# Dealing the two groups of head pairs in turn over the slots of a recurrent mixer

## The chip, the core and the metric

The kernel runs on one core of a Trainium2 chip. The core has five engines with a queue each: TensorE (PE in the profile, with its weight loads as PEld), VectorE (DVE), ScalarE (ACT), GpSimd (POOL) and SyncE (SP), which here only issues DMAs. Each engine works through its instructions in a fixed order and stands where one has to wait. The metric is the time of one execution on the device, in microseconds (us).

## What is computed

A trunk of two layers over 256 tokens of width 1024. Each layer runs three token mixers on the same normalised input and merges them:

```python
for l in range(DEPTH):
    h = rmsnorm(x, norm_g[l])
    proj = h @ w_in[l]
    (a_q, a_ff, a_fb, a_i, a_g, b_q, b_k, b_v, b_g, c_s, c_g, merge) = jnp.split(proj, IN_OFFSETS, axis=-1)
    y_a = hgrn2_mixer(a_q, a_ff, a_fb, a_i, lbs[l], hgrn_norm_g[l]) * silu(a_g)    # A: 8 heads of 128
    y_b = retention_mixer(b_q, b_k, b_v, ...) * silu(b_g)                          # B: 8 heads, values of 256
    y_c = rwkv7_mixer(c_s, ...) * silu(c_g)                                        # C: 16 heads of 64
    gates = sigmoid(merge.reshape(b, t, 3, D_MODEL))
    mixed = (gates[:, :, 0] * (y_a @ w_branch_a[l]) + gates[:, :, 1] * (y_b @ w_branch_b[l])
             + gates[:, :, 2] * (y_c @ w_branch_c[l]))
    x = x + mixed @ w_out[l]
return rmsnorm(x, final_norm_g)
```

A and C are gated recurrences in both directions; B is retention with a fixed decay. None of the three reads another's result before the merge.

## The kernel before

**Weights.** All weights come in blocks of 1024 x 256, each in two halves (`load_w`, L177). A half is loaded by SP (tile `wr`, L182), ACT casts it to a high part (`wh`, L184), DVE subtracts to get the low part (`wl`, L187), and PE multiplies three products of high and low parts (`feat_mm` L200, `tok_mm` L210). Each of wr, wh and wl has three buffers. A projection (`proj`, L213) goes into one of two PSUM buffers, called pj; it stays there until it has been read.

**C** is worked by pairs of heads. `c_prep` (L306) projects the blocks rk and vg and builds the products within the chunks (`c_Z`), `c_solve` (L403) inverts small blocks with a long row of short DVE instructions (L425 to L444), and `c_scan` (L450) carries the state through the chunks. `c_scan` of pair p runs two pairs behind `c_prep`.

**A** is worked by pairs of heads (`a_pair` L556): five projections (aff, afb, aq, ai, ag), then two heads (`a_head` L592), one behind the other. A head is a chain of decays on DVE and ACT (L595, L631 to L633), products on POOL and DVE (`a_sl`, L608 and L609), small matmuls (`a_p`) and masked copies on DVE into `a_pt` (L642, L659); its end is `a_o` (L664), its norm and gate (`a_rs`, L670, L671).

**B** is worked by pairs of heads (`b_pair` L689): bq and bk are projected into `b_z`, copied with halves swapped into `b_sw` by two DMAs, rotated by POOL (L698) and DVE (L699, L700). Each of the two heads then projects bv and bg, multiplies scores (`b_s`), weighs them (`b_pm`, L714), multiplies them with `b_v` and normalises (L724 to L739). A pair of B has six blocks of weights, a pair of A five, a pair of C two.

A and B share most of their buffers, by tags: s_0 (`a_ex` or `b_z`), s_1 (`a_lf` or `b_sw`), s_v (`a_v` or `b_v`), s_g (the gates), s_tmp and s_p (`a_pt` or `b_pm`) with one buffer each, s_e and a_sl with two, and one PSUM buffer, "ab". `a_kq` belongs to A alone, `b_gt` takes a_sl.

**Constants.** A takes five masks (`a_c`, loaded by `for_a` L676), B the cosines and sines of its rotation (`b_c`, loaded by `for_b` L680). Both have the tag ab_c with one buffer, so that `b_c` takes the place of `a_c`.

**The order.** The loop over p (L815) runs over the C pairs, from -2 to 7. In each turn, a slot here, it writes out `c_scan` of pair p, `c_prep` and `c_solve` of pair p + 2, and the pair of A or B that the table FILL (L26) names for this slot. The program that builds the kernel then orders the instructions of each engine: earlier text has precedence, but an instruction whose inputs or buffers are not ready is passed by later ones, by the builder's own estimate of times. So the work of a slot reaches into the next. On the chip this order is fixed.

**The merge** (`tail`, L752) follows the loop: gates and branch products of A, then of B, then of C, and the output projection (`wo`). It is a row of projections on PE.

Of the kernel before, what the change touches and what calls it, by code (L numbers as in the profile page):

```python
# [25 lines left out]
FILL = {-1: ("A0",), 0: ("A1",), 1: ("A2",), 2: ("A3",), 3: ("B0",), 4: ("B1",), 5: ("B2",), 6: ("B3",)}  # L26
# [6 lines left out]
# columns of a layer's packed parameters  # L33
# [9 lines left out]
# columns of the shape constants  # L43
# [9 lines left out]
# of the masks that A takes, and of the rotation that B takes  # L53
# [4 lines left out]
# blocks of weights in a layer, in the order of _blocks()  # L58
# [3 lines left out]
def _blocks():  # L62
    """(key, matrix, row range start, list of (column start, width)) of each block of 1024 rows and 256 columns."""
    r = [("codes", "w_in", 0, [(11264 + 3072, 256)])]
    for p in range(8):
        r.append((("rk", p), "w_in", 0, [(11264 + 128 * p, 128), (11264 + 1024 + 128 * p, 128)]))
        r.append((("vg", p), "w_in", 0, [(11264 + 2048 + 128 * p, 128), (14592 + 128 * p, 128)]))
    for p in range(4):
        for n, o in (("aff", 1024), ("afb", 2048), ("aq", 0), ("ai", 3072), ("ag", 4096)):
            r.append(((n, p), "w_in", 0, [(o + 256 * p, 256)]))  # L70
    for p in range(4):
        r.append((("bq", p), "w_in", 0, [(5120 + 256 * p, 256)]))
        r.append((("bk", p), "w_in", 0, [(6144 + 256 * p, 256)]))
        for h in (2 * p, 2 * p + 1):
            r.append((("bv", h), "w_in", 0, [(7168 + 256 * h, 256)]))
            r.append((("bg", h), "w_in", 0, [(9216 + 256 * h, 256)]))
    for m in range(3):
        for b in range(4):
            c = 256 * b
            r.append((("mg", m, b), "w_in", 0, [(15616 + 1024 * m + c, 256)]))  # L80
            for n, w, r0 in ((("wa", "w_branch_a", 0),), (("wb0", "w_branch_b", 0), ("wb1", "w_branch_b", 1024)),
                             (("wc", "w_branch_c", 0),))[m]:
                r.append(((n, b), w, r0, [(c, 256)]))
    for b in range(4):
        r.append((("wo", b), "w_out", 0, [(256 * b, 256)]))
    return r
# [8 lines left out]
def trunk(ctx: ExitStack, tc, x, wb, pp, lora, cst, gtab, ng, out, parts="ABCT", layers=L, dbg=None):  # L95
# [10 lines left out]
    # x and what its norm takes come before the other constants  # L106
# [27 lines left out]
    def ring(pool, shape, dt, tag, n, name):  # L134
        """a tile in the next of a tag's n buffers, in turn"""
        i = turn[tag] = (turn.get(tag, -1) + 1) % n
        return pool.tile(shape, dt, tag=f"{tag}{i}", bufs=1, name=name)
# [5 lines left out]
    DP = []  # L143
    for l in range(L):
        d = keep.tile([128, 26 + 8 + 8 + 32], F32, name=f"dp{l}")
        p = P_[l]
        mu = p[:, PO["mu"]:PO["mu"] + 52]
        # 1 - mu0 - mu1
        V.tensor_add(d[:, 0:26], mu[:, 0:26], mu[:, 26:52])
        V.tensor_scalar(d[:, 0:26], d[:, 0:26], -1.0, 1.0, op0=ALU.mult, op1=ALU.add)  # L150
        V.tensor_scalar(d[:, 26:34], p[:, PO["kk"]:PO["kk"] + 8], -1.0, None, op0=ALU.mult)
        V.tensor_scalar(d[:, 34:42], p[:, PO["ka"]:PO["ka"] + 8], -1.0, 1.0, op0=ALU.mult, op1=ALU.add)
        V.tensor_scalar(d[:, 42:74], p[:, PO["w0"]:PO["w0"] + 32], -1.0, None, op0=ALU.mult)
        DP.append(d)

    # lower bounds: softmax over the layers with its maximum, cumulated, less the first
# [13 lines left out]
    # cumsum - p[0]  # L170
# [6 lines left out]
    def load_w(l, key):  # L177
        """the parts of a block's halves"""
        W = []
        for h in range(2):  # L180
            raw = ring(wp, [128, 1024], F32, "wr", RW[0], "wr")
            nc.sync.dma_start(raw, wb[2 * (l * NBLK + BK[key]) + h])  # L182
            hi = ring(wp, [128, 1024], F32R, "wh", RW[1], "wh")
            S.copy(hi, raw)  # L184
            lo = ring(wp, [128, 1024], F32R, "wl", RW[2], "wl")
            n = WS[h]
            V.tensor_sub(lo[:, 0:n], raw[:, 0:n], hi[:, 0:n].bitcast(F32))  # L187
            if n < 1024:
                G.tensor_sub(lo[:, n:], raw[:, n:], hi[:, n:].bitcast(F32))
            W.append((hi, lo))  # L190
        return W

    def feat_mm(o, W, f, h, first=True, last=True):
        """o[feature, t] (+)= W[:, f*128:+128]^T h; half f of the block holds these columns"""
        whi, wlo = (t.rearrange("p (k c) -> p k c", c=128) for t in W[f])
        hhi, hlo = h
        n = 0
        for k in range(KT):
            for a, b in ((whi, hhi), (whi, hlo), (wlo, hhi)):
                PE.matmul(o, a[:, k], b[:, k, :], start=(first and n == 0), stop=(last and n == 3 * KT - 1))  # L200
                n += 1

    def tok_mm(o, W, t, h):
        """o[t, column] = h[:, t-tile]^T W; a half of the block holds four k-tiles"""
        hhi, hlo = h
        n = 0
        for k in range(KT):
            whi, wlo = (w.rearrange("p (k c) -> p k c", c=256)[:, k % 4] for w in W[k // 4])
            for a, b in ((hhi, whi), (hlo, whi), (hhi, wlo)):
                PE.matmul(o, a[:, k, t * 128:(t + 1) * 128], b, start=(n == 0), stop=(n == 3 * KT - 1))  # L210
                n += 1
# [8 lines left out]
    def sigmoid_of_exp(t):  # L220
        """t = exp(-x) -> sigmoid(x), in place; Ln ends at 2^64, where sigmoid(x) = 1 / t to the last bit"""
# [8 lines left out]
    def silu_from(pool, src, shape, tag, tmp, bufs=1, tb=1):  # L230
        """silu of a projection in PSUM"""
# [8 lines left out]
    def norm_T(xs, ss, gb, pool):  # L240
        """xs and the sums of its squares by token; gb: the gains, on every partition"""
# [21 lines left out]
    # ================= C: RWKV-7 =================  # L263
    pers = {}

    def c_setup(pool):
        """tiles whose blocks off the diagonal stay zero"""
# [27 lines left out]
    def c_codes(l, pool):  # L295
# [3 lines left out]
        # tanh(x) = 2 sigmoid(2 x) - 1  # L299
# [5 lines left out]
    def c_prep(l, p, codes, pool):  # L305
        """Everything of pair p up to the chunk products, evacuated and masked."""  # L306
# [13 lines left out]
        # normalised kk, negated  # L320
# [8 lines left out]
        # decay and a  # L329
# [21 lines left out]
        # its ninth block holds the stacked identity  # L351
# [4 lines left out]
        # bonus: sum of r k_d r_k over both directions  # L356
# [7 lines left out]
        # k~, beta~, alpha~, r~ of each direction, and the products within its chunks  # L364
# [6 lines left out]
        for d in range(2):  # L371
            # a chunk's blocks of 64: A_rk^T, r~, A_ak, A_rb^T, beta' (first alpha~), A_ab^T, k', diag g, alpha~^T
# [30 lines left out]
    def c_solve(l, p, st, pool):  # L403
        """Inverses of the diagonal 32 x 32 blocks of I - A_ab, one block and every fourth column a partition."""
# [17 lines left out]
        # inverses of the diagonal 4 x 4 blocks, in place: entry (i, k) of block I at 132 I + 32 k + i  # L422
# [8 lines left out]
        # this block's columns  # L431
        V.tensor_mul(tp, at(m, 0, (132, 8), (1, 4), (32, 4)), cc("hot")[:, None, None, :].to_broadcast([128, 8, 4, 4]))
        V.tensor_reduce(at(w, 0, (36, 8), (1, 4)), tp, axis=AX.X, op=ALU.add)
        # then four rows at a time
# [15 lines left out]
    def c_scan(l, p, st, pool, ydst):  # L450
# [10 lines left out]
        # v of each direction, transposed  # L461
# [18 lines left out]
        # (I - A_ab)^-1 [A_ak, alpha~^T] by blocks of 32, for a direction's four chunks at a time  # L480
# [14 lines left out]
        # what a chunk makes of its v and of the state before it: mt its output, mk the state after it  # L495
# [19 lines left out]
        # the state from chunk to chunk  # L515
# [24 lines left out]
        # group norm over a head's 64 partitions  # L540
# [14 lines left out]
    # ================= A: HGRN2 =================  # L555
    def a_pair(l, p, pool, ydst):  # L556
# [6 lines left out]
        # k = (1 - lb) sigmoid(-x), f = lb + (1 - lb) sigmoid(x); the first layer's lb is p[0] - p[0] = 0  # L563
# [28 lines left out]
    def a_head(l, hd, le, kq, v, g, pool, ydst):  # L592
        # decay sums within 128 positions: forward, and backward negated
# [10 lines left out]
        def pairs(e, s):  # L604
            """K (lower forward, upper backward) and Q (lower backward, upper forward), scaled"""
# [6 lines left out]
        # between the two tiles of 128  # L612
# [30 lines left out]
        # within 8 positions, from their middle  # L643
# [16 lines left out]
        # output, its norm over the 128 partitions and the gate  # L660
# [15 lines left out]
    def for_a(pool):  # L676
        only["A"] = t = pool.tile([128, 640], F32, tag="ab_c", bufs=1, name="a_c")
        nc.sync.dma_start(t, cst[:, NCST:NCST + 640])

    def for_b(pool):  # L680
        only["B"] = t = pool.tile([128, 2, T], F32, tag="ab_c", bufs=1, name="b_c")
# [6 lines left out]
    # ================= B: retention =================  # L688
# [52 lines left out]
    # ================= merge and output =================  # L741
# [64 lines left out]
    # ================= layers =================  # L806
# [40 lines left out]
def _consts():  # L847
# [31 lines left out]
    # [head, j, j-tile * 256 + i]  # L879
# [7 lines left out]
def _pack(inputs):  # L887
# [4 lines left out]
    for l in range(L):  # L892
        for n, (key, mat, r0, cols) in enumerate(_blocks()):
            m = np.concatenate([a[mat][l, r0:r0 + 1024, c0:c0 + w] for c0, w in cols], 1)
            if key[0] in TOK:
                # halves of four k-tiles
                m = m.reshape(2, 4, 128, 256).transpose(0, 2, 1, 3)
            else:
                # halves of 128 columns
# [3 lines left out]
    def tiles(v):  # L903
        """a vector of n * 128 values as [128, n]"""
# [40 lines left out]
```

## Time and profile before

| | before |
|---|---|
| median of three runs (1819.37 to 1822.58) | 1821.67 us |
| span of the profiled execution, first to last instruction | 1821.9 us |
| mean granted TensorE clock | 0.965 |
| DVE, weights' low parts (L187) | 372 instructions, 475.9 us |
| ACT, weights' high parts (L184) | 372 instructions, 388.4 us |

The span of the profiled execution serves as its own time. Busy time is the time in which an engine works on at least one instruction. Matmuls are pipelined, and the trace models their ends, so that a PE that shows busy need not be at its peak. In the views, a row of the windows holds a stretch (from:to, in us from the span's start), its length, the busy time of PE, PEld, DVE, ACT and POOL with the number of instructions, the granted clock of PE (1.00 is full), the busy share of the DMA engines and GB/s. A row of the timeline holds start, length, engine, line, operation, output and inputs, and in brackets the idle time before it and what ended that. A row of the waits holds who waited for whom, the total in us, the times, and the longest. A row of a tile's instructions holds the shortest, median and longest duration in ns, and the first and last start in us.

### The profile page before, as it was taken

Reading aid. Unit: us, or ns where it says so; the run is one execution under the profiler, and the core shown is the slowest. Engines: PE = TensorE matmul, PEld = TensorE weight load, DVE = VectorE, ACT = ScalarE, POOL = GpSimd, SP = SyncE. Lnnn points to the kernel's source line nnn. Section 1 sums busy time; section 2 is a strip of 40 time slices with the busy share of each in tenths; the row PEclk is TensorE's granted clock in tenths of the full one; section 3 lists DMA queues with packets and bytes.
Section 4 is the critical chain, followed back from the end, with each engine's and each line's share of the span. In section 5 each row is a group of like instructions: output and inputs, shape, how many; then the busy total and the mean of one; then the engine's idle time right before and its main releaser. Section 6 shows DMA issues by size and latency. Waiting matters only on the chain.

```text
span 1821.9 us, 33791 instructions
## 1 busy us (share of the span) xinstructions
PE 1667.6 (92%) x12960; PEld 1625.0 (89%) x12960; DVE 1415.4 (78%) x2597; ACT 1056.5 (58%) x1940; POOL 322.0 (18%) x312
## 2 busy tenths in 40 slices
PE   6888899999999999999888789988999999999997
PEld 6877899898999998999888788988889999999997
DVE  5799898998878785565657989989998787846554
ACT  5665566757465545555556556757573656456453
POOL 1122222212120200010011222223131202100100
PEclk9989999999999999999988889999999999999999
DMA  6333223324344443755533233233244444437653
GB/s 221 116 118 105 79 96 102 117 86 138 119 155 141 146 148 133 244 200 187 198 114 118 99 100 91 88 109 107 93 133 125 144 142 154 142 131 245 208 186 116
DMA packets 127873, 250.30 MB, mean 137 GB/s; under 512 B 62304, under 2 KB 66784, under 8 KB 127456
## 3 DMA queue, kind: packets, MB, share of 16 engines
q1 hardware_dynamic: 127712, 248.15, 41.6%
q8 instruction: 102, 1.67, 0.4%
q14 instruction: 59, 0.48, 0.1%
HBM read 229.22 MB, written 14.68 MB: 134 GB/s over the span
## 4 chain that ended last, share of the span: by engine, by line
PE 49%; DVE 30%; issue 7%; DMA 6%; ACT 4%; SPq 2%; POOL 0%; DVEq 0%; ACTq 0%; POOLq 0%
PE t_o L200 10%; PE p_mg L200 8%; DVE wl L187 7%; DVE c_tq L439 3%; PE p_bv L210 3%; PE p_vg L200 3%; PE p_bg L200 2%; DMA c_M<-s 2%; PE pj L210 2%; PE c_p L393 2%; DMA s<-c_Z 2%; ACT wh L184 2%; DVE c_ts L441 2%; PE p_rk L200 1%; PE c_p L395 1%
## 5 line engine op out<-in xcount | busy, mean ns | idle before, releaser
L187 DVE TENSOR_TENSOR wl<-wr,wh 128x1024 fp32r<-128x1024 f32 x372 | 475.9, 1280 | 192.3 <-ACT wh L184 190.9
L184 ACT CAST wh<-wr 128x1024 fp32r<-128x1024 f32 x372 | 388.4, 1045 | 272.7 <-PE t_o L200 56.2
L200 PE MATMUL t_o<-yh,wh 128*128 128x256 f32 x512 | 144.7, 284 | 2.8 <-ACT yh L748 2.8
L200 PE MATMUL t_o<-yl,wh 128*128 128x256 f32 x512 | 145.0, 284 | 0.5 <-DVE yl L749 0.5
L200 PE MATMUL t_o<-yh,wl 128*128 128x256 f32 x512 | 144.6, 283 | 0.0
L608 POOL TENSOR_TENSOR a_sl<-a_kq,a_e 128x256 f32<-128x256 f32 x80 | 80.9, 1015 | 230.9 <-ACT a_e L618 66.0
L200 PE MATMUL p_mg<-h_hi,wh 128*128 128x256 f32 x384 | 109.6, 285 | 0.0
L200 PE MATMUL p_mg<-h_hi,wl 128*128 128x256 f32 x384 | 109.4, 285 | 0.0
L200 PE MATMUL p_mg<-h_lo,wh 128*128 128x256 f32 x384 | 108.7, 283 | 0.0
L200 PEld LDWEIGHTS t_o<-yh,wh 128*128 128x128 f32 x512 | 97.6, 191 | 3.2 <-ACT yh L748 3.2
L200 PEld LDWEIGHTS t_o<-yl,wh 128*128 128x128 f32 x512 | 97.9, 191 | 1.0 <-DVE yl L749 0.9
L200 PEld LDWEIGHTS t_o<-yh,wl 128*128 128x128 f32 x512 | 97.9, 191 | 0.0
L393 PE MATMUL c_p<-c_Z,bbd 128*128 128x192 f32 x256 | 68.9, 357 | 29.7 <-DVE bbd L388 25.0
L439 DVE TENSOR_TENSOR c_tq<-W,c_M 128x16 f32<-128x16 f32 (+6 forms) x112 | 89.0, 795 | 1.4
L200 PE MATMUL p_vg<-h_hi,wh 128*128 128x256 f32 x256 | 78.1, 305 | 8.1 <-ACT c_k L288 4.1
L399 ACT COPY c_Z<-c_p 128x192 f32<-128x192 f32 x128 | 40.3, 318 | 74.9 <-DVE c_Z L396 73.7
L200 PE MATMUL p_bg<-h_hi,wl 128*128 128x256 f32 x256 | 75.0, 293 | 4.6 <-DVE wl L187 4.6
L210 PE MATMUL p_bv<-wh,h_hi 128*128 128x256 f32 x256 | 76.1, 297 | 1.1 <-ACT b_z L694 1.1
L210 PE MATMUL p_bv<-wl,h_hi 128*128 128x256 f32 x256 | 75.4, 295 | 1.7 <-DVE wl L187 1.7
L200 PE MATMUL p_vg<-h_lo,wh 128*128 128x256 f32 x256 | 75.8, 296 | 0.0
L200 PE MATMUL p_vg<-h_hi,wl 128*128 128x256 f32 x256 | 75.6, 295 | 0.0
L210 PE MATMUL p_bv<-wh,h_lo 128*128 128x256 f32 x256 | 74.7, 292 | 0.0
(334 smaller groups left out, 5983.3 us busy)
## 6 DMA issues: line engine op xcount, KB each, us to landing
wr<-in_wb_dram SPq DMA_DIRECT2D x372, 512.0 KB, 3.3
c_M<-s SPq DMA_DIRECT2D x64, 128.0 KB, 2.7
c_lt<-in_lora_dram SPq DMA_DIRECT2D x16, 256.0 KB, 2.7
b_sw<-b_z SPq DMA_DIRECT2D x16, 256.0 KB, 3.9
b_gt<-in_gtab_dram SPq DMA_DIRECT2D x16, 256.0 KB, 3.4
yb<-b_y SPq DMA_DIRECT2D x16, 256.0 KB, 3.0
yr<-yb SPq DMA_DIRECT2D x8, 512.0 KB, 5.0
s<-c_Z SPq DMA_DIRECT2D x128, 16.0 KB, 1.9
```

Source lines behind the costliest of these rows:

```text
L184: S.copy(hi, raw)
L187: V.tensor_sub(lo[:, 0:n], raw[:, 0:n], hi[:, 0:n].bitcast(F32))
L200: PE.matmul(o, a[:, k], b[:, k, :], start=(first and n == 0), stop=(last and n == 3 * KT - 1))
L210: PE.matmul(o, a[:, k, t * 128:(t + 1) * 128], b, start=(n == 0), stop=(n == 3 * KT - 1))
L393: PE.matmul(o[:, 2:5], bbd[:, c], z[:, c, 1:8:3], start=True, stop=True)
L395: PE.matmul(o[:, 0:6:5], kbd[:, c], z[:, c, 1:8:6], start=True, stop=True)
L399: S.copy(z[:, c, 4:9:2], o[:, 4:7])
L439: V.tensor_mul(tp, W[:, 0:n, None, 0:j].to_broadcast([128, n, 4, j]), M[:, 0:j, j:j + 4].rearrange("p j i -> p i j")[:, None].to_broadcast ...
L441: V.tensor_reduce(sm, tp, axis=AX.X, op=ALU.add)
L608: G.tensor_mul(s5[:, :, :, 0], k5[:, 0:2, :, 0], e5[:, :, :, 0])
```

## The change

FILL deals A and B in turn. Before, slots -1 to 2 hold A0 to A3 and slots 3 to 6 hold B0 to B3; now they hold A0, B0, A1, B1, A2, B2, A3, B3. `a_c` and `b_c` get tags of their own, so that both stay in SBUF for a layer (2560 and 2048 bytes of a partition, where 2560 served both). The scratch space for dynamic DMAs, which is taken from SBUF as well, is set to 1024 in place of its default. Comments are dropped; line numbers stay.

```diff
-FILL = {-1: ("A0",), 0: ("A1",), 1: ("A2",), 2: ("A3",), 3: ("B0",), 4: ("B1",), 5: ("B2",), 6: ("B3",)}
+FILL = {-1: ("A0",), 0: ("B0",), 1: ("A1",), 2: ("B1",), 3: ("A2",), 4: ("B2",), 5: ("A3",), 6: ("B3",)}
...
     def for_a(pool):
-        only["A"] = t = pool.tile([128, 640], F32, tag="ab_c", bufs=1, name="a_c")
+        only["A"] = t = pool.tile([128, 640], F32, tag="a_c", bufs=1, name="a_c")
         nc.sync.dma_start(t, cst[:, NCST:NCST + 640])
...
     def for_b(pool):
-        only["B"] = t = pool.tile([128, 2, T], F32, tag="ab_c", bufs=1, name="b_c")
+        only["B"] = t = pool.tile([128, 2, T], F32, tag="b_c", bufs=1, name="b_c")
         nc.sync.dma_start(t, cst[:, NCST + 640:NCST + 1152].rearrange("p (a t) -> p a t", a=2))
...
-    nc = _bacc.Bacc("TRN2", target_bir_lowering=False, num_devices=1)
+    nc = _bacc.Bacc("TRN2", target_bir_lowering=False, num_devices=1, dynamic_dma_scratch_size=1024)
```

The builder orders each engine anew. Three places show what moves. The first is SP's queue in layer 0, after the blocks of C's pair 0 have come back (`w`); `s` are C's small blocks on their way out to DRAM.

```order
 L455 DMA w_170<-s_571 32x8x32 x4
-L182 DMA wr<-in_wb_dram 128x1024 x2
-L672 DMA ya<-a_rs 128x256
-L182 DMA wr<-in_wb_dram 128x1024 x4
+L695 DMA b_sw<-b_z 64x1024
+L696 DMA b_sw<-b_z 64x1024
+L672 DMA ya<-a_rs 128x256
+L182 DMA wr<-in_wb_dram 128x1024 x5
+L709 DMA b_gt<-in_gtab_dram 128x512
+L182 DMA wr<-in_wb_dram 128x1024
+L709 DMA b_gt<-in_gtab_dram 128x512
 L410 DMA s_1828<-c_Z 32x4x32 x4
```

Between the same two steps of C, the weights that follow are now those of B0 in place of A1, and B0's swaps and decay tables have joined them.

The second place is DVE in layer 0, while A0's second head is worked beside `c_solve` of pair 1. Before:

```order
L432 TENSOR_TENSOR c_tp<-c_M,cst 128x128
L609 TENSOR_TENSOR a_sl<-a_kq,a_e 128x2x4x32
L222 TENSOR_SCALAR s_tmp<-s_tmp 128x512
L433 TENSOR_REDUCE W<-c_tp 128x8x4
L388 SCALAR_TENSOR_TENSOR bbd<-c_nkk,c_xw 64x4x64 x2
L187 TENSOR_TENSOR wl<-wr,wh 128x1024
L439 TENSOR_TENSOR c_tq<-W,c_M 128x16
```

Of the change:

```order
L699 TENSOR_TENSOR b_z<-b_z,b_c 128x1024
L609 TENSOR_TENSOR a_sl<-a_kq,a_e 128x2x4x32
L433 TENSOR_REDUCE W<-c_tp 128x8x4
L388 SCALAR_TENSOR_TENSOR bbd<-c_nkk,c_xw 64x4x64 x2
L439 TENSOR_TENSOR c_tq<-W,c_M 128x16
L609 TENSOR_TENSOR a_sl<-a_kq,a_e 128x2x8x16
L700 TENSOR_TENSOR b_z<-b_z,b_sw 128x1024
```

The rotation of B0 (L699, L700) now stands among the steps of A0's second head, where the silu of A1's query (s_tmp, L222) stood; L700 takes POOL's product `b_sw`, five instructions behind L699.

The third place is DVE where A0's second head ends (L670, `a_rs`). Before:

```order
L670 SCALAR_TENSOR_TENSOR a_rs<-a_o,pp_78,a_rs 128x256
L442 TENSOR_TENSOR c_tq<-c_ts,c_M 128x28x4
L187 TENSOR_TENSOR wl<-wr,wh 128x1024
L538 TENSOR_TENSOR c_os<-c_os,c_oc 128x256
L396 TENSOR_TENSOR c_Z<-c_p_1810,cst 128x2x2x64
L444 TENSOR_REDUCE W<-c_tq 128x7x4
L396 TENSOR_TENSOR c_Z<-c_p_1816,cst 128x2x2x64
L609 TENSOR_TENSOR a_sl<-a_kq,a_e 128x2x4x32
```

Of the change:

```order
L670 SCALAR_TENSOR_TENSOR a_rs<-a_o,pp_78,a_rs 128x256
L442 TENSOR_TENSOR c_tq<-c_ts,c_M 128x28x4
L444 TENSOR_REDUCE W<-c_tq 128x7x4
L236 TENSOR_TENSOR s_g<-p_bg,s_tmp 128x512
L538 TENSOR_TENSOR c_os<-c_os,c_oc 128x256
L396 TENSOR_TENSOR c_Z<-c_p_1810,cst 128x2x2x64
L396 TENSOR_TENSOR c_Z<-c_p_1816,cst 128x2x2x64
L714 TENSOR_TENSOR b_pm<-b_s,b_gt 128x512
```

Where the next head of A went on (`a_sl`), the gate of B0's first head (L236) and its scores (L714) now follow, both in buffers that A's head has just given back (s_g and s_p). This hand-over from A to B came once in a layer before, at A3 and B0, and now comes four times.

## The prediction

> **What bounds the kernel now.** The page's first part gives the whole span, its third the DMA queues.
>
> ```profile
> span 1821.9 us, 33791 instructions
> PE 1667.6 (92%) x12960; PEld 1625.0 (89%) x12960; DVE 1415.4 (78%) x2597; ACT 1056.5 (58%) x1940; POOL 322.0 (18%) x312
> q1 hardware_dynamic: 127712, 248.15, 41.6%
> ```
>
> TensorE (PE) is busy 92%, VectorE (DVE) 78%, and the DMA engines 42%: DMA volume is no bound. An average over stages says little more, so I cut the span where the work changes. The timeline of PE gives the first matmul of A1, of B0 and of the merge in each layer; the third and last rows are the tile view's and the timeline's for p_mg.
>
> ```profile
> 125.75 0.28 PE L200 MATMUL p_aff<-h_hi,wh 128*128 128x256 f32 x1
> 406.99 0.36 PE L200 MATMUL p_bq<-h_hi,wh 128*128 128x256 f32 x1 [0.43 <-DVE c_k L291]
> L200 PE MATMUL p_mg<-h_hi,wh x384: 274/283/469, 695.3 to 1782.3; 128*128 128x256 f32 x192
> 1031.26 0.36 PE L200 MATMUL p_aff<-h_hi,wh 128*128 128x256 f32 x1
> 1318.46 0.36 PE L200 MATMUL p_bq<-h_hi,wh 128*128 128x256 f32 x1
> 1605.37 0.36 PE L200 MATMUL p_mg<-h_hi,wh 128*128 128x256 f32 x1
> ```
>
> So in layer 0 the pairs A1 to A3 fill 126 to 407 and B0 to B3 fill 407 to 695; in layer 1, 1031 to 1318 and 1318 to 1605. The busy time in these four stretches, and in the merge of layer 0, with the granted clock:
>
> ```profile
> 126.00:407.00 281.00, 254.18 (x1971) 245.95 (x1969) 257.90 (x540) 174.27 (x357) 69.56 (x70) 0.97 0.32 99
> 407.00:695.00 288.00, 274.71 (x2111) 266.69 (x2112) 232.09 (x429) 164.19 (x313) 48.88 (x43) 0.98 0.44 140
> 1031.00:1318.00 287.00, 258.75 (x1957) 250.21 (x1956) 260.44 (x556) 178.65 (x361) 72.53 (x70) 0.94 0.32 100
> 1318.00:1605.00 287.00, 272.33 (x2126) 264.51 (x2127) 235.26 (x435) 163.72 (x312) 47.23 (x43) 0.99 0.44 139
> 695.00:880.00 185.00, 181.72 (x1508) 180.55 (x1507) 108.62 (x131) 101.56 (x135) 14.70 (x13) 1.00 0.56 194
> ```
>
> The columns after the length are PE, weight loads, DVE, ScalarE (ACT) and GpSimd (POOL). In A's stretches DVE is the fuller engine (257.90 / 281 = 91.8%, 260.44 / 287 = 90.7%) and PE has gaps (90.5%, 90.2%). In B's stretches it is the other way round: PE 95.4% and 94.9%, DVE 80.6% and 82.0%. The waits of DVE say the same; first the row of A's stretch of layer 0, then that of B's:
>
> ```profile
> DVE wl L187 <- ACT wh L184: 2.1, 2, 1.1
> ...
> DVE wl L187 <- ACT wh L184: 21.3, 15, 3.5
> ```
>
> In B's stretch DVE stands 21.3 us for the high part of the next weights, which waits for a buffer that PE still reads; in A's only 2.1 us. The merge (PE 98%) is PE's alone and is not touched.
>
> **The change part by part.** *The turns of A and B.* No instruction is added or removed; in each layer the fills of six of the eight slots are redealt (A0 and B3 stay). What can be won is the unlikeness of the stretches. Neighbours do share engines across a slot: though B0's projections begin at 407, its first v waits in PSUM until A3's last head has read A's v, at 469.
>
> ```profile
> L210 PE MATMUL p_bv<-wh,h_hi x256: 274/283/472, 418.1 to 1595.3; 128*128 128x256 f32 x128
> L705 ACT COPY b_v<-p_bv x16: 571/581/594, 469.4 to 1598.6; 128x512 f32<-128x512 f32 x16
> ```
>
> So work reaches some 60 us over a border, about as far as a slot is long (281 / 3 = 94 us for A, 288 / 4 = 72 us for B), and a heavy-DVE pair beside a heavy-PE pair should level the two.
>
> Four bounds, all from the rows of the stretches. Layer 0 needs 254.18 + 274.71 = 528.9 us of PE and 257.90 + 232.09 = 490.0 of DVE in 569 us; layer 1 needs 531.1 and 495.7 in 574.
> - PE full throughout as in B's stretches: 528.9 / 0.954 = 554.4 and 531.1 / 0.949 = 559.7, so 14.6 + 14.3 = **29 us** less.
> - Both engines together as full as in A's stretches (shares add up to 1.822 and 1.809): 1018.9 / 1.822 = 559.1 and 1026.8 / 1.809 = 567.6, so 9.9 + 6.4 = **16 us** less.
> - Both as full as in B's (1.760 and 1.769): 579.0 and 580.6, **17 us** more.
> - Only DVE bounds, at A's share: 490.0 / 0.918 = 533.9 and 495.7 / 0.907 = 546.2, **63 us** less.
>
> I take the middle of the first two, 22.6 us less: PE is the engine that fills up, and A's stretches are where both are well used.
>
> *The handovers.* From A to B the two share s_v, s_g, s_p and the one PSUM buffer "ab": B's bv and bg blocks sit in the two pj banks until A's second head is done, and behind them wait all projections, C's too. Before, that happens once in a layer, now four times: six more in all. (Back from B to A, a_ex waits for b_z's buffer as the next B pair's b_z did before: no new kind of wait.) Its price is read from the slot that has one against the next that has none, in each layer:
>
> ```profile
> 407.00:503.00 96.00, 90.52 (x674) 86.50 (x675) 82.76 (x165) 56.04 (x114) 19.77 (x18) 0.96 0.42 130
> 503.00:580.00 77.00, 73.28 (x582) 71.56 (x580) 59.26 (x113) 47.02 (x87) 12.87 (x12) 1.00 0.46 148
> ...
> 1318.00:1412.00 94.00, 88.08 (x685) 84.89 (x686) 86.86 (x172) 52.76 (x107) 18.68 (x18) 1.00 0.42 126
> 1412.00:1490.00 78.00, 74.40 (x576) 72.42 (x575) 58.69 (x107) 48.59 (x91) 11.99 (x12) 0.98 0.48 153
> ```
>
> PE stands 5.48 of 96 us (5.7%) with a handover and 3.72 of 77 (4.8%) without: 0.8 us more. In layer 1 it is 5.92 of 94 (6.3%) against 3.60 of 78 (4.6%): 1.6 us. The mean is 1.2, six of them 7.3 us. From above, the slot with a handover is 19 and 16 us longer, but DVE's 82.76 us against 59.26 show that most of that is A3's own work. Below nothing it could go only if a handover freed PE, which no row shows. I take 7.3, the nearest row.
>
> Here too belongs B's rotation, which now stands among A's heads on DVE (the second excerpt): L700 waits for POOL's product.
>
> ```profile
> L698 POOL TENSOR_TENSOR b_sw<-b_sw,b_c x8: 2366/2816/3466, 465.5 to 1573.3; 128x1024 f32<-128x1024 f32 x8
>   DVE b_z L700: 1.2, 1
> ```
>
> Before, eight such waits cost DVE 1.2 us in all, since the product had been made. If POOL is late with A's a_sl, the six moved ones cost up to 2.8 us each, 17 us on DVE. I take nothing beyond the handover's price, in whose slot these waits fall.
>
> *The constants.* b_c is loaded right behind a_c, ahead of fifteen weight loads on SP's queue (SyncE's), and never waits for A's masks.
>
> ```profile
> b_c<-in_cst_dram SPq DMA_DIRECT2D x2, 256.0 KB, 2.8
> ...
> SPq L682 <- DVE a_pt L659: 5.3, 1, 5.3
> ...
> POOL b_sw L698 <- DMA b_c<-in_cst_dram: 15.3, 1, 15.3
> ```
>
> What goes is one stand of SP's queue of 5.3 us, with C's lora weights and blocks behind it, and 15.3 us of POOL, which is 18% busy. What comes is at most 2.8 us at the start, ahead of the weights of the first pairs; in layer 1 the load lies in the merge, where DMA has room. Net nothing, within -5 and +3.
>
> *The scratch.* Every DMA that the page lists is issued by SP on q1, so the space given up has no user in the trace, and the tiles only move. Nothing; the merge, whose order is the same from its third block on, would show it.
>
> The sum: 22.6 - 7.3 = 15.3 us less. The span is 1821.9 and the median of the runs 1821.67, so nothing of note lies around the span and I count from 1821.9: **1807 us**, 0.8% less.
>
> **The rivals.** *DVE alone bounds, 1759.* PE's rows are busy from the start of a matmul to its modelled end, so a nearly full row may hide room. For it: the merge does 1508 matmuls in 185 us, 8.15 in a us, B's stretch only 2111 in 288, 7.33 (though these include C's, which take longer). At 8.15 the 4082 of both stretches would take 501 us, less than DVE's 533.9, and the fourth bound holds: 63 us less. Against it: PE's gaps in B's stretch are hardly there. The Trainium skill, Perfetto Trace Analysis (Identifying the Most-Contended Engine), takes matmul-busy time for a bad measure and goes by weight loads instead; these are busy 266.69 / 288 = 92.6% in B's stretch, and by them the first bound would be 31 us instead of 29, so the trace bears the rule out only a little.
>
> *The slots only change places, 1822.* The scheduler could spend each A slot on DVE and each B slot on PE as before, whatever the turn. For it: buffers let a fill run ahead by two blocks and two banks only. Against it: the 60 us of overlap above.
>
> *The handovers stop PE, 1834.* If all of PE's idle time in a slot with a handover (5.48 and 5.92 us, mean 5.7) is the handover's own, six cost 34 us, against 22.6: 11.6 us more. It decides from 3.8 us each (22.6 / 6). For it: the two banks are held for some 50 us (418 to 469). Against it: the slots without a handover idle nearly as much. With the third bound and 7.3 us it would be 1846.
>
> **How the numbers follow.** Forecast 0.47 (1790 to 1818), DVE alone 0.15, no change 0.12, handovers 0.26. A measurement of this kernel tells about 0.2%, 3.6 us, from no change. Faster is the first two, 0.62; same 0.12; slower 0.26. The range goes from 1770, between the forecast and the DVE rival, to 1846, the third bound with its handovers; it leaves out half of the DVE rival and the worst of the handovers, under 0.2.
>
> **What would show it.** Right: between A1's start and the merge, PE at 93 to 95% and DVE at 87 to 89% in every slot, some 7 us less in each layer, with the merge unchanged; DVE's wait for wh smaller than 21 us where B lies. The DVE rival: DVE over 90% there. No change: A slots at 91% DVE and B slots at 95% PE still alternate. Handovers: PE idle over 3.8 us more in each A to B slot, with waits of bv, bg or b_s behind a_rs, and L700 waiting for POOL. Wrong altogether: the last slots, where A3 now lies with little of C left, grow, or the merge changes.

## The result, and the profile after

The change makes the kernel slower: 1862.33 us (median of 4 runs, 1858.62 to 1863.67) against 1820.52 us (4 runs, 1815.17 to 1822.58), a ratio of 1.0234 [1.0215, 1.0254], in brackets its 95% interval. The prediction said 1807 us, and its range ended at 1846. Every ratio below is to the kernel before as it was measured beside that run; its median moved by 1.8 us between these measurements. The first lines of the page of after:

```profile
span 1861.9 us, 33787 instructions
PE 1679.0 (90%) x12960; PEld 1631.4 (88%) x12960; DVE 1419.1 (76%) x2597; ACT 1053.5 (57%) x1940; POOL 316.9 (17%) x312
```

The span is 40.0 us longer. PE has the same 12960 matmuls and is busy 11.4 us longer (1679.0 against 1667.6), so it idles 28.6 us more (182.9 against 154.3). DVE's busy time moves by 3.7 us. Nothing was added; PE waits more, and its work takes a little longer.

Where? I cut both spans at places that every order has: the first matmul of the rk block of C's pairs 2, 7, 10 and 15 (counted through both layers, from PE's timeline), and the store of the last head of B (`yb`, L739, from SP's timeline).

| stretch, us | before | after | difference |
|---|---|---|---|
| start to rk2 | 98.9 | 98.7 | -0.2 |
| rk2 to rk7 | 460.2 | 465.9 | +5.7 |
| rk7 to the last yb of layer 0 | 150.8 | 169.1 | +18.3 |
| to rk10 (merge, start of layer 1) | 293.2 | 292.3 | -0.9 |
| rk10 to rk15 | 465.9 | 458.3 | -7.6 |
| rk15 to the last yb of layer 1 | 150.6 | 178.7 | +28.1 |
| to the end (merge) | 202.3 | 198.9 | -3.4 |

The long middles of both layers change by -1.9 us together. The two ends, behind the last rk block, grow by 46.4. The windows show the same, first those of before (A1's first matmul to rk7, rk7 to the merge's first `t_o`, and the end of layer 1):

```profile
126.00:559.00 433.00, 398.88 (x3072) 385.55 (x3071) 381.74 (x765) 267.32 (x538) 99.95 (x98) 0.97 0.36 112
559.00:718.00 159.00, 151.40 (x1185) 147.85 (x1183) 121.16 (x228) 86.07 (x158) 21.35 (x18) 0.98 0.45 145
1469.00:1628.00 159.00, 150.85 (x1199) 146.85 (x1197) 120.85 (x232) 88.47 (x161) 20.92 (x18) 1.00 0.45 144
```

and those of after:

```profile
126.00:565.00 439.00, 398.93 (x3099) 387.86 (x3098) 373.65 (x752) 258.74 (x517) 92.69 (x86) 0.98 0.39 116
565.00:740.00 175.00, 158.85 (x1207) 152.44 (x1206) 132.38 (x248) 95.86 (x187) 31.86 (x30) 0.95 0.38 117
676.00:740.00 64.00, 53.60 (x372) 49.49 (x370) 34.09 (x64) 29.22 (x56) 7.21 (x8) 0.89 0.35 107
1484.00:1669.00 185.00, 164.92 (x1239) 157.69 (x1238) 136.90 (x260) 99.83 (x193) 31.39 (x30) 0.94 0.36 111
```

In the ends PE idled 7.6 and 8.2 us before; now 16.2 and 20.1. In layer 0 most of it lies in the last 64 us of the mixers, at a granted clock of 0.89. Idle time is half of the growth: of the 42 us by which the two windows are longer, PE idles 20.5 and is busy 21.5, with 62 more matmuls (1207 and 1239 against 1185 and 1199) and more time for each.

Why a late `yb` costs all that it is late is seen in SP's timeline (start, length, operation, output and input) at the end of layer 0, of before

```profile
709.92 0.33 SPq L739 DMA_DIRECT2D yb<-b_y  x1
710.29 0.42 SPq L747 DMA_DIRECT2D yr<-ya  x1
```

and of after:

```profile
733.74 0.33 SPq L739 DMA_DIRECT2D yb<-b_y  x1
734.12 7.90 SPq L747 DMA_DIRECT2D yr<-ya  x2
```

The merge's first load of finished heads (`yr`, L747) stands right behind the last store of heads, in both. The branch products, and with them all of the merge but the first projections of its gates, start when the last head of the mixers is stored, whatever PE has done by then.

What PE does just before, in after, is in its timeline (in brackets the idle time before a row, and what ended it). A3's second head is under way, and B3's `bv` and `bg` of the second head stand behind it:

```profile
675.50 0.28 PE L200 MATMUL p_bg<-h_hi,wl 128*128 128x256 f32 x1
...
680.02 0.66 PE L469 MATMUL c_vt<-cst,vtbd 128*128 128x128 f32 x4 [2.92 <-ACT vtbd L466]
680.51 0.64 PE L638 MATMUL a_p<-a_sl 128*128 128x128 f32 x4
683.65 1.20 PE L638 MATMUL a_p<-a_sl 128*128 128x128 f32 x4 [2.50 <-DVE a_pt L642]
...
687.99 1.19 PE L658 MATMUL a_p<-a_e 128*128 128x128 f32 x4 [1.33 <-DVE a_e L650]
...
698.78 0.47 PE L210 MATMUL p_bv<-wh,h_hi 128*128 128x256 f32 x1
```

and DVE's of the same kernel:

```profile
689.22 0.44 DVE L659 COPY_PREDICATED a_pt<-a_c,a_p 128x256 f32<-128x256 uint32 x1 [1.38 <-PE a_p L658]
690.98 0.44 DVE L659 COPY_PREDICATED a_pt<-a_c,a_p 128x256 f32<-128x256 uint32 x1 [1.31 <-PE a_p L658]
692.73 0.44 DVE L659 COPY_PREDICATED a_pt<-cst,a_p 128x256 f32<-128x256 uint32 x1 [1.31 <-PE a_p L658]
```

PE waits for DVE's copy and DVE for PE's next product, step by step: a head of A is a chain that by itself fills neither engine. From 676 to 688 us PE is busy 39% and DVE 87%, DVE also with the last steps of C's solve (L439 to L444); from 688 to 700 PE is busy 91%, with C's scan (`c_o`) besides, and DVE 23%. Elsewhere in the layer C's work and the projections fill most of such gaps (before, PE is busy 90% even in A's stretches). Here C's preparations are over and no projection runs for 23 us (676 to 699).

That leaves four suspects: the order itself (dealing in turn), the held projection banks, the buffer s_0 that A and B share, and A3's place in the last slots. Each experiment but the last two (h3 and h5) starts from the changed kernel.

### The profile page after: what moved, and what is told of

It is laid out like the page before. It is cut to its first block, busy times and chain, and to the rows that moved or that the text cites. A ratio compares the mean times of both kernels' runs of the same rounds, so it can differ in the third digit from the quotient of the medians.

```text
span 1861.9 us, 33787 instructions
## 1 busy us (share of the span) xinstructions
PE 1679.0 (90%) x12960; PEld 1631.4 (88%) x12960; DVE 1419.1 (76%) x2597; ACT 1053.5 (57%) x1940; POOL 316.9 (17%) x312
## 4 chain that ended last, share of the span: by engine, by line
PE 38%; DVE 36%; DMA 9%; issue 8%; ACT 5%; SPq 2%; POOL 1%; DVEq 0%; ACTq 0%; POOLq 0%
PE t_o L200 8%; DVE wl L187 8%; PE p_mg L200 5%; DVE c_tq L439 3%; PE pj L210 2%; PE p_rk L200 2%; ACT wh L184 2%; DVE c_ts L441 2%; DMA c_M<-s 2%; PE p_vg L200 2%; DMA yr<-yb 2%; DMA s<-c_Z 1%; PE p_bv L210 1%; PE p_afb L200 1%; PE c_p L393 1%
## 5 line engine op out<-in xcount | busy, mean ns | idle before, releaser
L439 DVE TENSOR_TENSOR c_tq<-W,c_M 128x16 f32<-128x16 f32 (+6 forms) x112 | 94.5, 844 | 1.8
L200 PE MATMUL p_bg<-h_hi,wh 128*128 128x256 f32 x256 | 75.5, 295 | 0.0
L200 PE MATMUL p_bg<-h_lo,wh 128*128 128x256 f32 x256 | 75.2, 294 | 0.0
L200 PEld LDWEIGHTS p_mg<-h_hi,wl 128*128 128x128 f32 x384 | 73.6, 192 | 1.8 <-DVE wl L187 1.8
```

The costliest lines, as they stand in the source:

```text
L439: V.tensor_mul(tp, W[:, 0:n, None, 0:j].to_broadcast([128, n, 4, j]), M[:, 0:j, j:j + 4].rearrange("p j i -> p i j")[:, None].to_broadcast ...
```

## Experiments

### Parts of the order

The first three put back parts of the old order, with the change's constants and scratch.

```diff
 slots:    -1  0  1  2  3  4  5  6
-FILL:     A0 B0 A1 B1 A2 B2 A3 B3   # the change
+FILL:     A0 A1 A2 A3 B0 B1 B2 B3   # e1_consts_only
+FILL:     A0 B0 A1 B1 A2 A3 B2 B3   # e2_a3_early
+FILL:     A0 A1 A2 B0 B1 B2 A3 B3   # e3_a3_late
```

> The turns of before (A0 A1 A2 A3 B0 B1 B2 B3) with the constants in two buffers and the smaller scratch. If the loss is in the turns (the end of the mixers, or the handovers): the time of before, 1820 within 5 us. If tags or moved tiles cost: near 1862.

Measured: 1829.23 us, ratio 1.0043 [1.0025, 1.0062], 4 us above the range expected for the turns and far from 1862.

> Turns A0 B0 A1 B1 A2 A3 B2 B3: as the change but for the last three, so that the mixers end on two B pairs as before, with two more handovers from A to B in a layer than before. Theory 'end' (A3 in slot 5, handing over to B3 where little of C is left): the 13 and 22 us between rk7 or rk15 and the merge go, and the time is 1815 to 1826. Theory 'handovers' (40 us over six, 6.7 each): four extra handovers, about 1847.

Measured: 1835.80 us, 1.0075 [1.0050, 1.0101], between the two expectations and in neither.

> Turns A0 A1 A2 B0 B1 B2 A3 B3: the order of before with A3 alone moved into slot 5. One more handover in a layer than before, at the end. Theory 'end': nearly the whole loss is there, 1850 to 1865. Theory 'handovers': two extra ones in all, about 1834.

Measured: 1856.71 us, 1.0192 [1.0168, 1.0216], as the theory of the end expected.

From e1 to e2, two of the three returns from B to A are put in, with two more handovers, and cost 6.6 us. From e2 to the change only A3 and B2 change places, in slots 4 and 5, and that costs 26.5. From e1 to e3 A3 moves to slot 5, with a single return: 27.5. So most of the loss goes with A3's slot.

### Held banks and shared buffers

e4 gives B's v and gate a buffer each of their own, f6 two each and `b_z` its own as well, f1 `b_z` alone; e7 has f6's two buffers with A first.

```diff
-qk = pool.tile([128, 2, 2, T], F32, tag="s_0", bufs=1, name="b_z")
+qk = pool.tile([128, 2, 2, T], F32, tag="b_z", bufs=1, name="b_z")        # f1, f6
-v = pool.tile([128, 2, T], F32, tag="s_v", bufs=1, name="b_v")
+v = pool.tile([128, 2, T], F32, tag="b_v", bufs=2, name="b_v")            # f6, e7 (e4: bufs=1)
-g = silu_from(pool, o, [128, 2, T], "s_g", "s_tmp")
+g = silu_from(pool, o, [128, 2, T], "b_g", "s_tmp", bufs=2)               # f6, e7 (e4: one)
```

> The change, with buffers of B's own for its v and its gate (one each), so that bv and bg leave the pj banks without waiting for A's second head. If the held banks make the loss: A1-to-merge shrinks, and the time falls to 1825 to 1840. If it is the amount of DVE work at the end (118 us busy of 149 against 108 of 136 before) or the bare chain of A3's head: 1855 or more.

Measured: 1864.31 us, 1.0240 [1.0219, 1.0262], the same as the change. B3's second `bv` and `bg` now run at 674 to 689 us, but then they sit in the two banks themselves, and the next block, the merge's first, starts only at 706. The hold has moved by one block.

> The change with b_z alone in a buffer of its own; the instructions stand in the same order on every engine as in the change. Theory 'shared s_0' (a pair of A after a pair of B begins late because a_ex cannot be written until the last b_s has read b_z): the 88 to 108 us from the end of a B pair to the end of A's next head shrink by some 35, 1815 to 1840 us. Theories 'hold' and 'A3 late': 1859 to 1865, the same as the change, since the order of the projections is what places A's pair.

Measured: 1858.88 us, 1.0222 [1.0194, 1.0250]. The instructions stand in the same order as in the change, so this run takes away one kind of wait and nothing else. It is worth some 3 us, and the intervals of the two kernels overlap. The shared s_0 is not the cause.

> The change with B's v and gate in two buffers of B's own and b_z in a buffer of its own, so that bv and bg of both heads of a B pair can leave the two pj banks while A's second head still runs. Theory 'hold' (bv7 and bg7 stand in the projections' line until A3's second head is done, 676 to 699 us in layer 0 and 1598 to 1627 in layer 1, and no work of C is left to fill PE): the two last holds of 23 and 29 us go, most of that comes off the end, 1815 to 1840 us. Theory 'A3 late' (the last A pair's own chain of heads, not the held banks, sets the last yb): under 10 us less, 1852 to 1865. Theory 'shared s_0': as for the next run, with what is gained there and no more.

Measured: 1843.45 us, 1.0145 [1.0111, 1.0179], between the two theories. The last hold is gone, and yet PE stands as long at the end. The window and PE's timeline of f6 at the end of layer 0:

```profile
685.00:735.00 50.00, 34.26 (x256) 31.52 (x254) 19.44 (x42) 20.38 (x40) 5.71 (x7) 0.88 0.38 127
```

```profile
734.91 0.80 PE L200 MATMUL t_o<-yh,wh 128*128 128x256 f32 x2 [13.11 <-ACT yh L748]
```

B3's projections now end at 685 instead of 713, but B3's heads still follow A3's, the last yb comes at 725.2, and PE stands before the first branch product `t_o` instead of before `p_bv`. What f6 won lies ahead of rk7 and rk15, where the other holds were: 465.9 to 450.0 us from rk2 to rk7, 458.3 to 447.0 from rk10 to rk15.

> A first as before (with the change's constants and scratch), and B's v and gate in two buffers of B's own: the control to the first run. Theory 'hold': there is one handover in a layer, with C beside it, so under 8 us less than the 1829 us of the same order without these buffers: 1821 to 1830. If dealing in turn is good in itself once no bank is held, the first run is under this one; if 'A3 late' holds, the first run is over 25 us above it.

Measured: 1818.17 us, 0.9989 [0.9971, 1.0006]. The buffers bring 11 us to A first too, a little more than was expected, and dealing in turn (f6) stays 25 us above it. Held banks were a part of the loss, not the main one.

### A3's place

All four have the two buffers of e7, and differ only in the table.

```diff
 slots:    -1  0  1  2  3  4  5  6
-FILL:     A0 B0 A1 B1 A2 B2 A3 B3   # the change and f6: A3 in slot 5, three returns from B to A
+FILL:     A0 B0 A1 B1 A2 A3 B2 B3   # e6_a3_early_two_bufs: A3 in slot 4, two returns
+FILL:     A0 B0 A1 B1 A2 B2 B3 A3   # k1_a3_last: A3 in slot 6, three returns
+FILL:     A0 A1 B0 A2 B1 A3 B2 B3   # l1_return_slot4: A3 in slot 4, two returns, the last to A3
+FILL:     A0 A1 A2 B0 B1 B2 A3 B3   # l2_one_return_slot5: A3 in slot 5, one return
```

> A0 B0 A1 B1 A2 A3 B2 B3, with B's v and gate in two buffers of B's own: two of the change's three returns from B to A stay, but A3 no longer lies in the last slots. Theory 'empty end' (what is lost is lost where A's last pair, a long chain of small steps, lies where C has little left): within 6 us of A first with the same buffers (1818), 1812 to 1825 us. Rival 'turns' (each return from B to A costs its share wherever it lies): two thirds of the 25 us by which dealing in turn with these buffers (1843) stood above A first with them, 1831 to 1839.

Measured: 1817.30 us, 0.9972 [0.9951, 0.9993]. Against f6 only A3 and B2 have changed places (f6 has `b_z`'s buffer besides, which in f1 left the order as it was and brought some 3 us): 26 us less.

> A0 B0 A1 B1 A2 B2 B3 A3, with B's v and gate in two buffers of B's own: A3 one slot later still than in the change, with three returns from B to A as there, and three handovers instead of four. Theory 'empty end' (A's pair takes some 115 to 130 us from its first projection to its end, and nothing but the wait for it is left): the time goes on growing with A3's slot, 1817 us in slot 4, 1843 in slot 5, now 1850 to 1875. Rival 'turns' (the returns and handovers, not the place): 1835 to 1843.

Measured: 1843.61 us, 1.0114 [1.0089, 1.0139]: a miss for the theory of the empty end, which expected more than f6's 1843. Its trace suggests why: in both, one pair of A and one of B are left behind C's last projection (vg7, which ends at 572 us in both), and the last store of a head comes at 725.2 in f6 and 724.6 in k1. Which of the two is last made no difference. But the result also fitted the rival, so two more runs had to tell them apart.

> A0 A1 B0 A2 B1 A3 B2 B3, with B's v and gate in two buffers of B's own: two returns from B to A, the last of them to A3 in slot 4, with B2 and B3 behind C's last projections as in A first. Theory 'place' (A3's pair costs only where C's last projections are done before it): 1810 to 1825 us, like A first with these buffers (1818). Rival 'return' (the last return to A costs 26 us wherever it lies, since a pair of A that follows one of B starts from its first projection): 1835 to 1848.

Measured: 1815.66 us (10 runs), 0.9974 [0.9962, 0.9987].

> A0 A1 A2 B0 B1 B2 A3 B3, with the same buffers: one return, to A3 in slot 5. Theory 'place': 1835 to 1850 us, the same as dealing in turn with these buffers (1843), though there is one return in place of three. Rival 'number of returns': a third of 25 us over A first (1818), 1823 to 1831.

Measured: 1845.41 us, 1.0131 [1.0108, 1.0153].

This decides it. A return right before A3 shows no cost while A3 lies in slot 4; with a single return the time is 27 us above e7 when A3 lies in slot 5. The windows from the end of vg7 to the first `t_o` in layer 0 show what is different, of l1, l2 and f6, one after the other:

```profile
568.00:716.00 148.00, 140.67 (x1094) 136.22 (x1093) 115.60 (x215) 83.20 (x155) 27.01 (x23) 0.99 0.44 137
```

```profile
576.00:734.00 158.00, 141.39 (x1118) 135.97 (x1118) 120.44 (x229) 92.08 (x179) 32.28 (x30) 0.99 0.38 117
```

```profile
572.00:735.00 163.00, 139.79 (x1111) 134.64 (x1109) 121.01 (x230) 92.05 (x181) 31.56 (x31) 0.96 0.39 123
```

PE has 140 to 141 us of work there in all three. Where two pairs of B are left (l1) it idles 7.3 us (148 - 140.67); where a pair of A and one of B are left, 16.6 (l2) and 23.2 (f6). The change idles 16.2 of 157 there. The idle time is not the whole difference, and it is not the same in both layers: in layer 1 PE idles 10.3 (l1), 14.1 (l2) and 23.0 us (f6) in this stretch. From e7 to l2 the stretch holds all of the loss: it grows by 18.0 and 11.6 us in the two layers, and the spans differ by 26.9. From e6 to f6 it grows by 11.4 and 4.0 us, and the spans differ by 19.8; where the rest lies stays open.

### One slot earlier

g1 is the change with every fill one slot earlier (-2 to 5), h2 the same with the two buffers, h1 the same buffers and slots with A first.

```diff
 slots:    -2 -1  0  1  2  3  4  5  6
-FILL:        A0 B0 A1 B1 A2 B2 A3 B3   # the change
+FILL:     A0 B0 A1 B1 A2 B2 A3 B3      # g1_slot_early, h2_slot_early_two_bufs
+FILL:     A0 A1 A2 A3 B0 B1 B2 B3      # h1_a_first_early_two_bufs
```

> The change with every fill one slot earlier (A0 in slot -2 to B3 in slot 5), so that A3 and B3 lie beside C's last preparation and solve. Theories 'hold' and 'A3 late' both need the last slots to be empty of C: 1825 to 1845 us, with PE busy over 95% in the 150 us before the merge. Theory 'serial chain' (the heads of A and B follow each other through single buffers all the way from the first slot, so that the end is set by their sum): within 5 us of the change, 1857 to 1867, since the chain begins no more than some 5 us earlier.

Measured: 1837.25 us, 1.0102 [1.0076, 1.0127], 25 us less than the change. With C's last preparation beside A3 the end is cheaper; a chain that ran through the whole layer would have left the time as it was.

> The change one slot earlier (A0 in slot -2 to B3 in slot 5), with B's v and gate in two buffers of B's own. Theory 'empty end': the 25 us that one slot earlier brought and the 15 us that the buffers brought are partly the same idle PE, 1815 to 1830 us. Rival 'turns': the three returns remain whole, 1835 to 1845. If C's scans, which now end last, set the end of the merge, the time is not under 1830 either, and the branch products of C wait for them.

Measured: 1826.35 us, 1.0019 [1.0002, 1.0037], as the theory of the empty end expected.

> A first, one slot earlier (A0 in slot -2 to B3 in slot 5), with B's v and gate in two buffers of B's own: the control to the run before it, and a candidate to be faster than both kernels. 'Empty end': little is idle at the end of A first (B3 lies there), so 1808 to 1822 us, and at most 10 under the 1818 of A first in its old slots. If C's scans end last: 1822 to 1835.

Measured: 1856.74 us, 1.0184 [1.0151, 1.0216], far over both expectations. SP's timeline of h1 in layer 0 shows that C now ends last:

```profile
682.68 0.33 SPq L739 DMA_DIRECT2D yb<-b_y  x1
...
768.08 0.33 SPq L553 DMA_DIRECT2D yc<-c_os  x1
769.48 10.48 SPq L747 DMA_DIRECT2D yr<-yb  x2
```

B's last store is 27 us earlier than before, but C's last store (`yc`) comes at 768, and a load of `yb` stands behind it in the queue. Before, C's last store comes 36 us behind B's (745.7 and 709.9); here it is 85 us. How much of the 39 us above e7 comes from this stays open.

### Constants and scratch

h3 is the kernel before with the scratch alone; h5 adds the two buffers to it and keeps the one tag for both constants.

```diff
-nc = _bacc.Bacc("TRN2", target_bir_lowering=False, num_devices=1)
+nc = _bacc.Bacc("TRN2", target_bir_lowering=False, num_devices=1, dynamic_dma_scratch_size=1024)   # h3, h5
```

> The kernel before with the scratch of dynamic DMAs set to 1024 and nothing else; the order of every engine is that of before. If the 8 us that the change's constants and scratch cost with A first (1829 against 1820) come from the scratch, 1825 to 1831 us; if they come from the constants' own tags and the order that follows from these, 1817 to 1824.

Measured: 1819.04 us, 0.9974 [0.9959, 0.9989]. The scratch costs nothing.

> The kernel before (A first, one tag for the constants of A and B), with B's v and gate in two buffers of B's own and the scratch at 1024, for which SBUF has no room otherwise. If the 10 us between A first with own tags for the constants (1829) and the scratch alone (1819) are the price of the order that the own tags bring, and the 11 us that the buffers brought there (1818) are separate from it: 1805 to 1812 us, faster than both kernels. If the buffers only took back what the own tags had cost: 1815 to 1821.

Measured: 1829.05 us, 1.0039 [1.0025, 1.0053]: outside both expectations. With A first there are now four kernels: neither own tags nor buffers 1819.0 (h3), own tags 1829.2 (e1), buffers 1829.1 (h5), both 1818.2 (e7). Each edit alone costs 10 us, and both together nothing. So neither has a fixed price. DVE's order is that of before in h3 and another one in each of e1, h5 and e7, so the likely reading is that each edit sets the builder on another order and that an order is worth some 10 us either way. That the order is the cause is not shown, and which rows of it cost the time was not tried.

## Why the prediction was wrong, point by point

The runs put the loss together in three steps: from before to e1 (constants, with the order that they bring) 8.7 us, from e1 to e2 (turns, A3 still in slot 4) 6.6, from e2 to the change (A3 to slot 5) 26.5; in all 41.8.

- **The turns, 22.6 us less. This step failed, and twice.** First, it expected PE to fill up where the pairs alternate ("PE full throughout as in B's stretches", 95%). PE did not. From rk2 to rk7 and from rk10 to rk15 it is busy 91.0% and 90.5% before, 89.8% and 90.7% in the change and, without holds, 91.4% and 91.1% in f6 and 90.0% and 91.6% in l1. These middles do get shorter, by 29.1 us in f6, the size of the first bound, and by 39.0 in l1, but mostly because less of PE's work lies in them. The windows of the two middles, first of before, then of l1:

```profile
98.90:559.10 460.20, 418.59 (x3212) 404.93 (x3211) 408.77 (x821) 282.77 (x568) 109.94 (x106) 0.96 0.36 112
1003.10:1469.00 465.90, 421.62 (x3201) 408.21 (x3200) 415.58 (x838) 284.75 (x569) 110.01 (x106) 0.95 0.35 110
98.80:547.20 448.40, 403.75 (x3110) 391.46 (x3109) 394.96 (x783) 269.24 (x544) 101.00 (x98) 0.97 0.37 114
1003.90:1442.50 438.60, 401.77 (x3085) 389.21 (x3084) 392.64 (x796) 268.59 (x537) 101.06 (x95) 0.96 0.37 113
```

PE has 34.7 us less to do in l1's middles (805.5 against 840.2). C's blocks come earlier there, and work of A and B is left for the ends. Second, the step took the layer as if it ended when PE's total is done. The middles end with C's blocks, the layer with the last heads of A and B: in l1 the ends are 11.2 + 18.8 = 30.0 us longer, with 27.7 us more of PE's work. What l1 gains against A first with the same buffers is 2.5 us (1815.66 against 1818.17), and their intervals overlap.
- **A3's place had no term.** "The last slots, where A3 now lies with little of C left, grow" stood in the prediction only as what would make it wrong altogether, without a price and without a share of the chances. It measured 26.5, 27.5, 26.2 (f6 - e6) and 27.2 us (l2 - e7), 1.4 to 1.7% by the ratios: four times about the same, with and without buffers, after one return and after three. The rows of before held a hint: A's stretches filled DVE and left gaps in PE, and the last 4 slots were B's.
- **The handovers, 7.3 us more: the right size.** Freeing the banks (f1 to f6) brought 15.4 us for eight handovers, 1.9 each where 1.2 was taken, and PE's idle time in the two middles, where six of them lie, falls by 11.6 us from the change to f6 (90.0 to 78.4). A new order alone can move 10 us, so this is no exact price. The rival in which handovers stop PE (34 us for six) did not come about, and the third bound with handovers (1846), nearest to the result, gave no reason for its shares. From rk2 to the last yb the shares of PE and DVE in the change do add up to 1.74 and 1.75, near that bound's 1.76 (before: 1.78), but the bound names no wait.
- **Back from B to A, "no new kind of wait": right as to the buffer** (f1, some 3 us), and in l1 a return shows no cost while C has work left. It was the slot, not the return.
- **B's rotation behind POOL: right.** In after, DVE's waits hold one of 2.2 us in the whole span, where up to 17 us had been thought possible. DVE's wait for the weights' high part is 19.9 us between 126 and 714 us, hardly smaller than before (21.3 and 2.1 us in the two stretches of layer 0), and in layer 1 it is 16.4 against 15.4: no levelling is seen in it.

```profile
DVE wl L187 <- ACT wh L184: 19.9, 18, 3.0
...
DVE b_z L700 <- POOL b_sw L698: 2.2, 1, 2.2
```

- **The constants, nothing within -5 and +3:** e1 measured 8.7 us more than before. The transfers were weighed; that another tag gives another order was not. **The scratch, nothing:** right (h3).
- **The merge unchanged: right.** From the last yb to the end of layer 1 it takes 198.9 us, before 202.3.
- **The signs that were named:** PE at 93 to 95% and DVE at 87 to 89% from A1 to the merge. The window to rk7 has PE at 90.9% (398.93 / 439) and DVE at 85.1%, both lower than before (92.1% and 88.2%).

Of all the orders l1 is the fastest, 0.26% under before and so ahead of both kernels. h3, which has the order of before, shows the same ratio, so this is no proof that dealing in turn helps.

## What to carry to other kernels

Where independent rows of work fill each other's gaps, look first at what is left when the filler ends: the job with the longest chain and the least PE work (here a pair of A) belongs where filler remains, and the dense one (a pair of B) last. Busy shares over a stage bound a gain only if the last row to end gets shorter with them; take as the end what the next stage waits for (here the last store of a head), and forecast that. A stretch that got shorter has gained nothing if its work only moved: compare the work in it as well as its length. And where a builder orders the instructions, an edit that should cost nothing can bring 10 us through a new order: run it in two surroundings before giving it a price.

## What the runs showed of the hardware

PE's granted clock falls where PE has gaps. Four windows of after, 12 us each, around the last hold:

```profile
652.00:664.00 12.00, 11.90 (x97) 11.51 (x95) 9.52 (x24) 7.37 (x17) 5.05 (x3) 1.00 0.44 133
664.00:676.00 12.00, 9.90 (x68) 9.46 (x68) 11.73 (x19) 3.14 (x7) 2.41 (x4) 0.86 0.32 102
676.00:688.00 12.00, 4.62 (x25) 3.53 (x23) 10.49 (x19) 7.36 (x15) 3.93 (x5) 0.76 0.34 98
688.00:700.00 12.00, 10.94 (x59) 10.19 (x60) 2.71 (x5) 2.83 (x6) 0.00 (x0) 0.67 0.25 64
```

The granted clock falls to 0.86, 0.76 and 0.67, though PE never stands longer than 2.92 us before an instruction here, and the matmuls that run then take longer. PE's timeline has them 0.21 us apart at 673 us and 0.12 us apart at 699:

```profile
673.66 0.41 PE L200 MATMUL p_bg<-h_hi,wl 128*128 128x256 f32 x1
673.88 0.41 PE L200 MATMUL p_bg<-h_hi,wh 128*128 128x256 f32 x1
...
699.20 0.28 PE L210 MATMUL p_bv<-wl,h_hi 128*128 128x256 f32 x1
699.32 0.28 PE L210 MATMUL p_bv<-wh,h_hi 128*128 128x256 f32 x1
```

How much of the 11.4 us more of busy time comes from this is not shown. Idle time alone does not set it: f6 idles 177.1 us in all and is busy only 1660.7, less than before, and h3, in the order of before, is busy 1662.3 against 1667.6. The Trainium skill, TensorE: Matmul & The Clock Gate (Part 1: The HAM clock gate), says that the array drops to half its rate after an idle window and comes back after a busy one; the spacing agrees with it, near enough (0.21 against 0.12).

A second thing is small: h3 has the order of before and differs from it only in the size of the scratch, and so in addresses in SBUF, and yet it measured 0.26% faster, with an interval (0.9959 to 0.9989) that does not hold 1. Between kernels that stand that close, the runs here do not tell a cause.
